# Attention probabilities laid out by key block, the sink as a column, reciprocals as a power on GpSimd: a Hymba-style streaming step in float32

## The chip, the core and the metric

One core of a Trainium2 chip runs one launch of the kernel. The metric is the device time of that launch in microseconds (us); lower is better. The engines are named as in the profile: PE is TensorE (PEld its weight loads), DVE is VectorE, ACT is ScalarE, POOL is GpSimd, SP is SyncE, which issues most DMAs. All data is float32, and 320 rows (256 of a prompt and 64 of a running stream) pass through one layer.

## The reference, cut to what matters

```python
z = rmsnorm(x, ln_g) @ w_in                      # 2048 -> 1024 q, 128 k, 128 v, 1024 u, 1024 v of the gating
# group A: 16 heads of 64, 2 key heads; a chunk of 64 queries sees its own 64 keys and the 128 before
s = einsum('...qhgd,...khd->...hgqk', q, k) * HEAD_DIM ** -0.5 + bias
sink = sinks[..., None]                          # one learned number per head
m = maximum(max(s, axis=-1), sink)
p = exp(s - m[..., None])
w = p / (sum(p, axis=-1, keepdims=True) + exp(sink - m)[..., None])
o = einsum('...hgqk,...khd->...qhgd', w, v)
# group B: spatial gating over chunks of 128 positions, 8 channel groups
u, v = gelu(zs)[..., :1024], rmsnorm(gelu(zs)[..., 1024:], g)
sp = einsum('gij,bnjgc->bnigc', masked w_s, v) + b_s
s_o = u * sp
# finish
x = x + concat(rmsnorm(o, g_a), rmsnorm(s_o, g_s)) @ w_out
y = x + square(relu(rmsnorm(x, ln_ffn) @ w_up)) @ w_down        # 2048 -> 8192 -> 2048
```

The outputs are `y` and the new rows of keys, values and of the normalised gating `v`.

## The kernel before

**Products.** Activations lie with channels on the 128 partitions and the 320 rows along the free dimension. Each product of a weight matrix is made by `products`: a step loads four 128 x 256 blocks of weights (`w_raw`), ACT copies them rounded to `w_hi` (line 115), DVE subtracts to get the rest, `w_lo` (line 116), and PE adds up three products for each block, high x high, high x low and low x high (line 141): 24 matmuls of 128x128 by 320 columns. `w_hi` and `w_lo` have three buffers each. The same split is made of the activations (`XH`, `XL` and so on). The stages follow each other: q and k, v of the attention (with the sums of squares `ssq` of the input, lines 285 to 292), the other q heads, the gating's `v` in four groups, its `u` in four groups, `w_out`, `w_up` and `w_down`.

**What stands between the steps.** `between_pieces` puts small work after a chosen step of a product. On PE it is pinned by `tc.issue_after`: the small matmuls stand behind the step's last matmul, and the next step stands behind them (`behind = narrow[-1]`). On the other engines a scheduler sets the order at build time; each engine then runs its list strictly in order.

**Attention.** A unit is one chunk of 64 queries for one key head, ten in all (5 chunks x 2 key heads; 64, 128 or 192 keys). `attend(i)` is called thirteen times (i = 0 to 12), every second step, and does one stage of three units at once:

- scores of unit i (`scores`, line 420): 8 products of 64x64 by 64 to 192 columns into two PSUM banks `s_ps`; then `softmax` on DVE, ACT and POOL;
- the transposes of the probabilities of unit i-2 (line 472) into two `misc` banks, from where DVE copies them to SBUF (`pts`, line 501);
- the values of unit i-3 (line 485): probabilities times values, 64x64 by 128 columns.

In `softmax` four DVE instructions scale and add the bias (line 434), DVE takes the maximum (438), joins the sink (440), negates (442) and forms sink minus maximum (444), ACT takes the exponent of that (445) and four exponents with row sums (449), DVE adds (451) and takes the reciprocal (452), and POOL multiplies the tile `s` in place (453). The tile `s` has two buffers. Probabilities are transposed in pieces of 128 rows x 128 columns that hold two key blocks; which value tiles they meet depends on the unit (`blocks`, with eight value tiles made by `values` from six transposes, line 349). A product of one key block and its partner in the same 128 rows lands in different places, so half of the results are added by DVE afterwards (line 497).

**Gating norm.** The channel factor `g_sv` of the gating's norm is multiplied on POOL into all 320 rows of `gv` (line 541), before the mixing matmuls (line 566); DVE then adds the bias `sgb` (line 571).

**Norm of q.** `norm_q` sums squares with four matmuls of 128x32 by 320 columns (line 323), sends the sums through DRAM to turn them, and raises to -0.5 on POOL (line 334).

Of the kernel before, what the change touches and what calls it, by code (L numbers as in the profile page):

```python
# [8 lines left out]
F32 = mybir.dt.float32  # L9
# [21 lines left out]
def hymba_step_kernel(ctx: ExitStack, tc: tile.TileContext, i, o):  # L31
# [53 lines left out]
    nc.gpsimd.dma_start(out=tab, in_=i["table"].rearrange("b h -> h b"))  # L85
    inv_1k = const.tile([P, 1], F32, name="inv_1k")
# [16 lines left out]
    loads, between, rests, steps, narrow, carry = [], [], [], [], [], []  # L103
# [18 lines left out]
    def products(w, k0, nk, c0, ps, rh, rl, deep=None, between_pieces={}, halves_behind={}):  # L122
# [6 lines left out]
        for a in range(0, nk, 4):  # L129
# [3 lines left out]
            with tc.issue_after(halves_behind[a // 4]()) if a // 4 in halves_behind else nullcontext():  # L133
                high, low = halves(raw, hi, lo)
# [166 lines left out]
    def evict_q(g, q_ps):  # L301
# [11 lines left out]
        nc.scalar.activation(out=sq, in_=qg, func=AF.Square)  # L313
        return sq

    q_dram = dram.tile([2, 2, 2, 2, T], F32, name="q_dram")
    r_at = lambda g, b, p: (g // 2) * 20 + p * 10 + (g % 2) * 5 + b

    def norm_q(h, sqs):

        st = misc()
        for c in range(4):
            mm = nc.tensor.matmul(out=st[c * 32:(c + 1) * 32, 0:T], lhsT=hone, rhs=sqs[c // 2][:, :, c % 2], start=True, stop=True)  # L323
# [14 lines left out]
    v0, v64, v128, vC, vD, w2, w3, w4 = (vz[:, x] for x in range(8))  # L338

# [4 lines left out]
    def values(*xs):  # L344
        for x, vps in zip(xs, [score_bank(1, "vps"), misc()] if len(xs) == 2 else banks(4)):
            t0 = (0, 64, 128, -64, 192, 256)[x]
            n = min(P, T - t0)
            with tc.issue_after(narrow[-1]):
                mm = nc.tensor.transpose(out=vps[0:n, 0:P], in_=kvx[:, 448 + t0:448 + t0 + n], identity=ident)
            narrow.append(mm.ins)  # L350
            for dst, r in (((v0, slice(0, P)), (w3, slice(HD, P))), ((v64, slice(0, P)),),
                           ((v128, slice(0, P)), (w2, slice(0, HD))), ((w2, slice(HD, P)),),
                           ((w3, slice(0, HD)), (vD, slice(HD, P))), ((w4, slice(0, HD)),))[x]:
                nc.vector.tensor_copy(out=dst[r], in_=vps[r, 0:P].rearrange("k (h d) -> k h d", h=2))


    q1_ps = product(w_in, 0, KT, 256, xh, xl, between_pieces={0: lambda: rstd(ssq, mean_dm, EPS, rx)},
                    halves_behind={2: lambda: rests[-1]})
# [5 lines left out]
    nc.scalar.activation(out=ksq, in_=zk, func=AF.Square)  # L364
    q0_sq = evict_q(0, q0_ps)
# [3 lines left out]
    def first_norms():  # L369
        rstd(ksq, mean_hd, EPS, rk)  # L370
        q1_sq.append(evict_q(1, q1_ps))

    def keys():
        for dst, c in ((kn[:, 0:256], slice(0, 256)), (kn[:, 384:448], slice(256, 320))):
            nc.vector.scalar_tensor_tensor(out=dst, in0=zk[:, c], scalar=g_k, in1=rk[:, c], op0=ALU.mult, op1=ALU.mult)
        for h in range(2):
# [8 lines left out]
        values(0, 1)  # L385

    q2_ps = product(w_in, 0, KT, 512, xh, xl,
                    between_pieces={0: first_norms, 1: lambda: norm_q(0, (q0_sq, q1_sq[0])), 2: keys, 3: lambda: values(2, 3, 4, 5)},
                    halves_behind={1: lambda: q0_out})
# [16 lines left out]
    room = blk("vnat", [P, 2432])  # L406
# [3 lines left out]
    pt1 = at.tile([P, 768], F32, name="pt1", bufs=1)  # L410
    pts = [(kzv[:, 1920:2304], room[:, 2048:2432]), (pt1[:, 0:384], pt1[:, 384:768])]
# [12 lines left out]
    def softmax(u, s_ps):  # L424
# [12 lines left out]
        m = at.tile([P, 2, 2], F32, name="m", tag="m")  # L437
        nc.vector.tensor_reduce(out=m, in_=sv, axis=AX.X, op=ALU.max)
        sk = sinks_pj[:, :, js]
# [310 lines left out]
```

## Time and profile before

| | |
|---|---|
| runs | 1239.65, 1239.93, 1240.73 us; median 1239.93 |
| profiled execution | 1239.04 us, of which 1237.3 are the span from first to last instruction |
| busy in the span | PE 1232.8 us, DVE 663.6, ACT 492.0, POOL 114.0 |
| granted TensorE clock | 1.0 throughout |
| DMA | 188.03 MB, mean 152 GB/s |

The span is cut into windows by the profile's time axis: the first product with q and k, v runs to about 34 us, the other q heads and the gating's `v` and `u` with the attention between them to about 212 us, and the rest is `w_out`, `w_up`, `w_down`. A row of the timeline has start and length in us, engine, line, operation, output<-input and shape; a bracket behind it is the time the engine sat idle before and what released it. In a group row (by line and shape) the numbers are busy us, mean ns of one, idle before. One matmul of float32 is listed as two records, a transpose and a matmul of the split operands as one.

### The profile page before, as it was taken

To read this page: it belongs to the slowest core of one execution; us is meant where nothing else is said; L and a number is where in the kernel's file an instruction comes from. 1 tells how busy PE (TensorE), PEld (TensorE's weight loads), DVE (VectorE), ACT (ScalarE), POOL (GpSimd) and SP (SyncE) were. 2 spreads that over 40 slices of the span, in tenths; PEclk is the share of its full clock that TensorE was granted. 3 is DMA by queue.
4 is the path that set the end of the run, shared out by engine and by line. 5 is a ranking of instruction groups with operands and counts; after the bars stand their busy time and mean duration, and the time that the engine had idled before them with its cause. 6 is when DMAs were issued, how large, how long until landed. Compare 5 with 4: busy or idle time off the path is not lost.

```text
span 1237.3 us, 20626 instructions
## 1 busy us (share of the span) xinstructions
PE 1232.8 (100%) x8666; PEld 1225.0 (99%) x8666; DVE 663.6 (54%) x796; ACT 492.0 (40%) x652; POOL 114.0 (9%) x139
## 2 busy tenths in 40 slices
PE   9999999999999999999999999999999999999998
PEld 9999999999999999999999999999999999999998
DVE  7877778877864444444444444444444434444343
ACT  7446566435534432333434332344432333433321
POOL 3127454102200000000000000000000000000000
PEclk9999999999999999999999999999999999999999
DMA  9753346444555444454444444455444454445540
GB/s 282 226 148 104 104 138 195 153 154 141 151 152 153 153 147 145 152 154 149 146 149 153 154 150 143 151 154 152 147 147 151 154 151 144 150 152 164 172 161 33
DMA packets 187934, 188.03 MB, mean 152 GB/s; under 512 B 7616, under 2 KB 187376, under 8 KB 187840
## 3 DMA queue, kind: packets, MB, share of 16 engines
q1 hardware_dynamic: 186544, 185.48, 48.7%
q0 software_dynamic: 864, 0.98, 0.4%
q8 instruction: 68, 1.11, 0.4%
q10 hardware_dynamic: 432, 0.24, 0.1%
q14 instruction: 26, 0.21, 0.1%
HBM read 183.10 MB, written 3.35 MB: 151 GB/s over the span
## 4 chain that ended last, share of the span: by engine, by line
PE 99%; DVE 0%; issue 0%; ACT 0%; DVEq 0%
PE acc L141 93%; PE q_ps L237 1%; PE misc L141 1%; PE acc L237 1%; PE s_ps L420 1%; PE misc L472 0%; PE misc L83 0%; PE misc L485 0%; PE s_ps L485 0%; PE g_ps L566 0%; PE misc L566 0%; PE misc L553 0%; PE misc L323 0%; ACT s L449 0%; ACT w_hi L115 0%
## 5 line engine op out<-in xcount | busy, mean ns | idle before, releaser
L116 DVE TENSOR_TENSOR w_lo<-w_raw,w_hi 128x1024 fp32r<-128x1024 f32 x332 | 416.0, 1253 | 422.7 <-ACT w_hi L115 414.1
L115 ACT ACTIVATE w_hi<-w_raw 128x1024 fp32r<-128x1024 f32 x332 | 351.8, 1060 | 670.9 <-PE acc L141 646.7
L141 PE MATMUL acc<-H2H,w_lo 128*128 128x320 f32 x1024 | 316.4, 309 | 0.0
L141 PE MATMUL acc<-H2H,w_hi 128*128 128x320 f32 x1024 | 316.4, 309 | 0.0
L141 PE MATMUL acc<-H2L,w_hi 128*128 128x320 f32 x1024 | 316.4, 309 | 0.0
L141 PE MATMUL acc<-FH,w_hi 128*128 128x320 f32 x992 | 306.5, 309 | 0.0
L141 PE MATMUL acc<-FL,w_hi 128*128 128x320 f32 x992 | 306.5, 309 | 0.0
L141 PE MATMUL acc<-FH,w_lo 128*128 128x320 f32 x992 | 306.5, 309 | 0.0
L141 PEld LDWEIGHTS acc<-H2H,w_hi 128*128 128x128 f32 x1024 | 192.2, 188 | 0.0
L141 PEld LDWEIGHTS acc<-H2L,w_hi 128*128 128x128 f32 x1024 | 192.2, 188 | 0.0
L141 PEld LDWEIGHTS acc<-H2H,w_lo 128*128 128x128 f32 x1024 | 192.2, 188 | 0.0
L141 PEld LDWEIGHTS acc<-FH,w_hi 128*128 128x128 f32 x992 | 186.2, 188 | 0.0
L141 PEld LDWEIGHTS acc<-FL,w_hi 128*128 128x128 f32 x992 | 186.2, 188 | 0.0
L141 PEld LDWEIGHTS acc<-FH,w_lo 128*128 128x128 f32 x992 | 186.2, 188 | 0.0
L141 PE MATMUL acc<-XH,w_hi 128*128 128x320 f32 x352 | 110.7, 314 | 0.0
L141 PE MATMUL acc<-XH,w_lo 128*128 128x320 f32 x352 | 108.8, 309 | 0.0
L141 PE MATMUL acc<-XL,w_hi 128*128 128x320 f32 x352 | 108.7, 309 | 0.0
L141 PEld LDWEIGHTS acc<-XH,w_hi 128*128 128x128 f32 x352 | 66.1, 188 | 3.1 <-issue 3.0
L141 PEld LDWEIGHTS acc<-XL,w_hi 128*128 128x128 f32 x352 | 66.1, 188 | 0.0
L141 PEld LDWEIGHTS acc<-XH,w_lo 128*128 128x128 f32 x352 | 66.1, 188 | 0.0
L658 DVE SCALAR_TENSOR_TENSOR tf<-acc,r 128x640 f32<-128x640 f32 x32 | 26.4, 824 | 41.8 <-PE acc L141 41.8
L673 DVE TENSOR_TENSOR xT<-xT,acc 128x640 f32<-128x640 f32 x31 | 25.5, 821 | 41.8 <-PE acc L141 41.8
(227 smaller groups left out, 1086.3 us busy)
## 6 DMA issues: line engine op xcount, KB each, us to landing
w_raw<-in_w_up SPq DMA_DIRECT2D x128, 512.0 KB
w_raw<-in_w_down SPq DMA_DIRECT2D x128, 512.0 KB
w_raw<-in_w_in SPq DMA_DIRECT2D x44, 512.0 KB
w_raw<-in_w_out SPq DMA_DIRECT2D x32, 512.0 KB
w_first<-in_w_in SPq DMA_DIRECT2D x14, 256.0 KB
out_yT<-xT SPq DMA_DIRECT2D x7, 320.0 KB
xT<-in_xT SPq DMA_DIRECT2D x8, 160.0 KB
xT<-in_xT SPq DMA_DIRECT2D x4, 320.0 KB
```

The source lines that it names most:

```text
L115: return (pin(nc.scalar.activation(out=hi, in_=raw, func=AF.Copy)).ins, pin(nc.vector.tensor_tensor(out=lo, in0=raw, in1=hi.bitcast(F32), ...
L116: pin(nc.vector.tensor_tensor(out=lo, in0=raw, in1=hi.bitcast(F32), op=ALU.subtract)).ins)
L141: mm = nc.tensor.matmul(out=out, lhsT=w_[:, k, g * P:(g + 1) * P], rhs=r_(kk), start=(kk == 0 and x == 0), stop=(kk == nk - 1 and x == 2))
L237: mm = nc.tensor.matmul(out=ps[:, 0:T], lhsT=w_[:, j, k, g * P:(g + 1) * P], rhs=r_(a + k), start=(a + k == 0 and x == 0), stop=(a + k == ...
L420: mm = nc.tensor.matmul(out=s_ps[p][x * HD:(x + 1) * HD, j * nk:(j + 1) * nk], lhsT=qT[hs, blk_, a + x], rhs=kz[hs, kv, k0:k0 + nk], start ...
L658: nc.vector.scalar_tensor_tensor(out=t, in0=ps[:, :, 0:T], scalar=0.0, in1=r2[:, None, :].to_broadcast([P, 2, T]), op0=ALU.max, op1=ALU.mult)
L673: nc.vector.tensor_tensor(out=xT[:, a, c], in0=xT[:, a, c], in1=p, op=ALU.add)
```

## The change

- **Probabilities by key block.** POOL writes the normalised probabilities to a new tile `pr`, laid out by key block (`p`, block `n`, head `j`, 64 keys), in two instructions for each unit. Each block is transposed by itself, separately for the two 64-query halves of the partitions: 64 rows x 128 columns in, 128 partitions x 64 columns out, the halves into two banks. The two value heads `j` then lie on the two halves of the partitions, so the values meet plain value tiles: 4 products for each key block, added up in one place for each `j`. The additions of line 497 go. The value tiles are seven, made from three transposes in one bank and four ACT copies (`values`, `values_out`) instead of six transposes and nine DVE copies; two DMAs instead of three bring the cached values.
- **The sink as a column.** `s` gets one more column that holds the sink; maximum (negated by the same instruction), exponent and row sum run over it. Lines 440, 442, 444, 445, 451 go; a DVE copy of 128x4 comes. `s` has one buffer instead of two.
- **Reciprocal.** A POOL power with exponent -1 (tile `minus`) replaces DVE's reciprocal.
- **Gating norm.** For the 256 prompt rows `g_sv` is no longer multiplied on POOL; DVE's addition of the bias becomes a multiply and add. For the 64 sample rows it stays on POOL.
- **Order.** Squares of the input start three steps earlier in the first product; the splits of the sums (`parts_x`, `parts_k`) are made ahead of the pieces that use them; `norm_q(1)` moves one step ahead, right behind `attend(2)`; the values of the first kind move to the piece of `norm_q(0)`.

```diff
-        with tc.issue_after(steps[min(8 + k // 2, 11)][0]):
+        with tc.issue_after(steps[min(5 + k // 2, 11)][0]):
...
-    def values(*xs):
-        for x, vps in zip(xs, [score_bank(1, "vps"), misc()] if len(xs) == 2 else banks(4)):
-            ...
-                mm = nc.tensor.transpose(out=vps[0:n, 0:P], in_=kvx[:, 448 + t0:448 + t0 + n], identity=ident)
-            ...
-                nc.vector.tensor_copy(out=dst[r], in_=vps[r, 0:P].rearrange("k (h d) -> k h d", h=2))
+    def values():
+        with tc.issue_after(narrow[-1]):
+            vps = score_bank(1, "vps").rearrange("k (x d) -> k x d", x=4)
+            for x, (t0, n) in enumerate(TT):
+                mm = nc.tensor.transpose(out=vps[0:n, x], in_=vT[:, t0:t0 + n], identity=ident)
+    def values_out():
+        for dst, to, of in ((low, 0, low), (high, 1, high), (high, 0, low), (low, 1, high)):
+            with tc.issue_after(turned[1]):
+                nc.scalar.activation(out=vz[dst, to:5:2].rearrange("k x h d -> k x (h d)"), in_=vps[of, 0:3 - to], func=AF.Copy)
...
-                    between_pieces={0: first_norms, 1: lambda: norm_q(0, (q0_sq, q1_sq[0])), 2: keys, 3: lambda: values(2, 3, 4, 5)},
+                    between_pieces={0: first_norms, 1: lambda: (values(), norm_q(0, (q0_sq, q1_sq[0])), values_out()), 2: keys},
...
-        s = at.tile([P, 2, 2, 192], F32, name="s", tag="s", bufs=2)
+        s = at.tile([P, 2, 2, 193], F32, name="s", tag="s", bufs=1)
+        sv, se = s[:, :, :, 0:nk], s[:, :, :, 0:nk + 1]
+        nc.vector.tensor_copy(out=s[:, :, :, nk], in_=sinks_pj[:, :, js])
         for p in range(2):
             for j in range(2):
                 nc.vector.scalar_tensor_tensor(out=sv[:, p, j], ...)
-        m = at.tile([P, 2, 2], F32, name="m", tag="m")
-        nc.vector.tensor_reduce(out=m, in_=sv, axis=AX.X, op=ALU.max)
-        nc.vector.tensor_tensor(out=m, in0=m, in1=sk, op=ALU.max)
-        nc.vector.tensor_scalar(out=nm, in0=m, scalar1=-1.0, scalar2=None, op0=ALU.mult)
-        nc.vector.tensor_tensor(out=es, in0=sk, in1=m, op=ALU.subtract)
-        nc.scalar.activation(out=es, in_=es, func=AF.Exp)
+        nc.vector.tensor_reduce(out=nm, in_=se, axis=AX.X, op=ALU.max, negate=True)
...
-                nc.scalar.activation(out=sv[:, p, j], in_=sv[:, p, j], func=AF.Exp, bias=nm[:, p, j:j + 1],
+                nc.scalar.activation(out=se[:, p, j], in_=se[:, p, j], func=AF.Exp, bias=nm[:, p, j:j + 1],
                                      accum_out=den[:, p, j:j + 1])
-        nc.vector.tensor_tensor(out=den, in0=den, in1=es, op=ALU.add)
-        nc.vector.reciprocal(out=den, in_=den)
-        ready[:] = [nc.gpsimd.tensor_tensor(out=sv, in0=sv, in1=den[:, :, :, None].to_broadcast([P, 2, 2, nk]),
-                                            op=ALU.mult).ins]
+        nc.gpsimd.tensor_tensor(out=den, in0=den, in1=minus, op=ALU.pow)
+        pr = at.tile([P, 2, 3, 2, HD], F32, name="pr", tag="pr", bufs=2)
+        for p in range(2):
+            ready[:] = [nc.gpsimd.tensor_tensor(out=pr[:, p, 0:ns].rearrange("x n j k -> x j n k"),
+                                                in0=sv[:, p].rearrange("x j (n k) -> x j n k", k=HD),
+                                                in1=den[:, p, :, None, None].to_broadcast([P, 2, ns, HD]), op=ALU.mult).ins]
...
+            def turn(p, n, x):
+                return nc.tensor.transpose(out=bank[x][:, (p * 3 + n) * HD:(p * 3 + n + 1) * HD],
+                                           in_=s[hs[x], p, n].rearrange("x j k -> x (j k)"), identity=ident[hs[x], hs[x]])
...
-                if va is not None:
-                    nc.vector.tensor_tensor(out=dst, in0=dst, in1=side[1 - j, j].rearrange("p (a q) -> p a q", a=2), op=ALU.add)
...
-            1: lambda: attend(2 * g + 2), 2: lambda: norm_q(1, (q2_sq, q3_sq)) if g == 0 else None,
-            3: lambda: attend(2 * g + 3)})
+            1: lambda: (attend(2 * g + 2), norm_q(1, (q2_sq, q3_sq)) if g == 0 else None), 3: lambda: attend(2 * g + 3)})
...
-            for dst, c in ((gv[:, a, 0:256], slice(0, 256)), (gvs[:, a], slice(256, T))):
-                with tc.issue_after(ready[0]) if g == 3 else nullcontext():
-                    nc.gpsimd.tensor_scalar(out=dst, in0=gv[:, a, c], scalar1=g_sv[:, a:a + 1], scalar2=None, op0=ALU.mult)
+            with tc.issue_after(ready[0]) if g == 3 else nullcontext():
+                nc.gpsimd.tensor_scalar(out=gvs[:, a], in0=gv[:, a, 256:T], scalar1=g_sv[:, a:a + 1], scalar2=None, op0=ALU.mult)
...
-            nc.vector.tensor_tensor(out=gv[:, g, 0:256].rearrange("p (b i) -> p b i", b=2),
-                                    in0=sp_ps[:, 0:256].rearrange("p (b i) -> p b i", b=2),
-                                    in1=sgb[:, g, None, :].to_broadcast([P, 2, P]), op=ALU.add)
+            nc.vector.scalar_tensor_tensor(out=gv[:, g, 0:256].rearrange("p (b i) -> p b i", b=2),
+                                           in0=sp_ps[:, 0:256].rearrange("p (b i) -> p b i", b=2), scalar=g_sv[:, g:g + 1],
+                                           in1=sgb[:, g, None, :].to_broadcast([P, 2, P]), op0=ALU.mult, op1=ALU.add)
```

On PE, `attend(10)` before: the last matmul of a step, six transposes of `s` in pieces of 128x128, the values (`pt` are transposed probabilities, `kzv` holds the value tiles) into four places, and the next step.

```order
L141 MATMUL acc<-XH,w_lo 128x320
L472 MATMUL misc<-ident,s 128x128 x6
L485 MATMUL misc<-pt_868,kzv 64x128 x2
L485 MATMUL s_ps_2096<-pt_868,kzv 64x128 x2
L485 MATMUL misc<-pt_868,kzv 64x128 x2
L485 MATMUL s_ps_2096<-pt_868,kzv 64x128 x2
L485 MATMUL s_ps_2095<-pt_868,kzv 64x128 x2
L485 MATMUL misc<-pt_868,kzv 64x128 x2
L141 MATMUL acc<-XH,w_hi 128x320
```

The same place now:

```order
L145 MATMUL acc<-XH,w_lo 128x320
L483 MATMUL misc<-ident,pr 128x64 x12
L493 MATMUL misc<-pt_856,kzv 64x128 x12
L145 MATMUL acc<-XH,w_hi 128x320
L145 MATMUL acc<-XL,w_hi 128x320
```

Twelve transposes with 64 columns out stand where six with 128 stood; the number of value products is the same, and they no longer touch the score banks. On DVE, around the softmax of unit 6 (128 keys; `z` and `gc` are the gelu's), before:

```order
L434 SCALAR_TENSOR_TENSOR s<-s_ps_1606,rq,bias 128x128 x2
L501 COPY kzv<-misc 128x384
L434 SCALAR_TENSOR_TENSOR s<-s_ps_1605,rq,bias 128x128 x2
L497 TENSOR_TENSOR ao<-ao,misc 128x2x64
L501 COPY vnat<-misc 128x384
L497 TENSOR_TENSOR ao<-ao,s_ps_1605 128x2x64
L438 TENSOR_REDUCE m<-s 128x4
L440 TENSOR_TENSOR m<-m,sinks 128x4
L442 TENSOR_SCALAR nm<-m 128x4
L444 TENSOR_TENSOR es<-sinks,m 128x4
L451 TENSOR_TENSOR den<-den,es 128x4
L452 RECIPROCAL den<-den 128x4
```

The same place now:

```order
L118 TENSOR_TENSOR w_lo<-w_raw,w_hi 128x1024
L444 COPY s<-sinks 128x4
L118 TENSOR_TENSOR w_lo<-w_raw,w_hi 128x1024
L447 SCALAR_TENSOR_TENSOR s<-s_ps_1582,rq,bias 128x128 x2
L447 SCALAR_TENSOR_TENSOR s<-s_ps_1583,rq,bias 128x128 x2
L451 TENSOR_REDUCE nm<-s 128x4
L506 COPY kzv<-misc 128x384 x2
L118 TENSOR_TENSOR w_lo<-w_raw,w_hi 128x1024
L444 COPY s<-sinks 128x4
```

The small instructions and the additions are gone; the copy of the sinks, which writes the only buffer of `s`, stands ahead of the next unit's four scalings, and both copies out of the transposes' banks stand behind those four. On POOL, units 3 and 4 (192 keys) before:

```order
L453 TENSOR_TENSOR s<-s,den 128x768
L334 TENSOR_TENSOR rq<-r_q,nhalf 128x20
L541 TENSOR_SCALAR gvs<-gv,cols 128x64 x2
L541 TENSOR_SCALAR gv<-gv,cols 128x256
L513 TENSOR_TENSOR acc_v<-acc_v,sq 128x320
L541 TENSOR_SCALAR gv<-gv,cols 128x256
L453 TENSOR_TENSOR s<-s,den 128x768
```

The same units now:

```order
L347 TENSOR_TENSOR rq<-r_q,nhalf 128x20
L545 TENSOR_SCALAR vnat<-gv,cols 128x64 x2
L457 TENSOR_TENSOR den<-den,minus 128x4
L519 TENSOR_TENSOR acc_v<-acc_v,sq 128x320
L461 TENSOR_TENSOR pr<-s,den 128x2x3x64 x2
L457 TENSOR_TENSOR den<-den,minus 128x4
L461 TENSOR_TENSOR pr<-s,den 128x2x3x64 x2
```

Each unit has a power and two multiplies in place of one multiply, and the power of unit 3 stands behind the `rq` power of `norm_q(1)`.

More of the change, by code (lines that the diff above doesn't have):

```diff
@@ L85, in hymba_step_kernel @@
     nc.gpsimd.dma_start(out=tab, in_=i["table"].rearrange("b h -> h b"))
+    minus = const.tile([P, 2, 2], F32, name="minus")
+    nc.vector.memset(minus, -1.0)
     inv_1k = const.tile([P, 1], F32, name="inv_1k")
@@ L100, in hymba_step_kernel @@
     nc.vector.memset(hone[HD:P, 1:2], 1.0)
-    loads, between, rests, steps, narrow, carry = [], [], [], [], [], []
+    firsts, loads, between, rests, steps, narrow, carry = [], [], [], [], [], [], []
     def load(out, in_):
@@ L405, in hymba_step_kernel @@
     probs, ready = {}, []
-    room = blk("vnat", [P, 2432])
+    room = blk("vnat", [P, 2560])
     vnat = room[:, 0:2048].rearrange("p (t c) -> p t c", t=2)
-    pt1 = at.tile([P, 768], F32, name="pt1", bufs=1)
-    pts = [(kzv[:, 1920:2304], room[:, 2048:2432]), (pt1[:, 0:384], pt1[:, 384:768])]
+    pts = [kzv[:, 1792:2560].rearrange("k (x p n q) -> k x p n q", x=2, p=2, n=3),
+           at.tile([P, 2, 2, 3, HD], F32, name="pt1", bufs=1)]
     def scores(u, s_ps):
@@ L460, in attend @@
         t, v = t if 0 <= t < 10 else None, v if 0 <= v < 10 else None
-        bank = [misc(), misc()] if t is not None else None
-        s_ps = [score_bank(p) for p in range(2)]
+        bank = [misc(), misc()] if t is not None else [score_bank(r) for r in range(2)]
+        s_ps = [score_bank(p) for p in range(2)] if i < 10 else None
+        hs = [slice(r * HD, (r + 1) * HD) for r in range(2)]
         def behind(mms):
@@ L468, in attend @@
         if t is not None:
-            s = probs.pop(t).rearrange("x p j k -> x p (j k)")
-            nk = blocks[units[t][0]][2]
-            cols = ((P, 2),) if nk == HD else ((0, 0), (192, 1)) if nk == P else ((0, 0), (256, 1), (P, 2))
-            behind([lambda p=p, x=x, c=c: nc.tensor.transpose(out=bank[p][:, x * P:(x + 1) * P], in_=s[:, p, c:c + P],
-                                                              identity=ident) for p in range(2) for c, x in cols])
+            s = probs.pop(t)
+            subs = range(len(blocks[units[t][0]][4]))
+            def turn(p, n, x):
+                return nc.tensor.transpose(out=bank[x][:, (p * 3 + n) * HD:(p * 3 + n + 1) * HD],
+                                           in_=s[hs[x], p, n].rearrange("x j k -> x (j k)"), identity=ident[hs[x], hs[x]])
+            behind([lambda p=p, n=n, x=x: turn(p, n, x) for p in range(2) for n in subs for x in range(2)])
         if i < 10:
@@ L477, in attend @@
             blk_, kv = units[v]
-            q0, va, vb = (blocks[blk_][x] for x in (0, 4, 5))
-            hs = [slice(r * HD, (r + 1) * HD) for r in range(2)]
-            side = {(r, j): bank[r][:, 384:512] if bank and j == 0 else s_ps[r][:, 384:512] if j else s_ps[r][:, 0:P]
-                    for r in range(2) for j in range(2)}
-            def part(r, j, p, span):
-                lhsT, c = (va[j][hs[r], kv], slice(j * P, (j + 1) * P)) if span < 2 else (vb[j][hs[j], kv], slice(256, 384))
-                return nc.tensor.matmul(out=side[r, j][hs[p]], lhsT=lhsT, rhs=pts[v % 2][p][hs[r], c],
-                                        start=span < 2 or va is None, stop=span == 2 or vb is None or r != j)
-            turns = [x for x in (0, 2, 1) if (va, va, vb)[x] is not None]
-            behind([lambda r=r, p=p, x=x: part(r, 1 - r if x == 1 else r, p, x) for x in turns for r in range(2) for p in range(2)])
+            q0, tiles = blocks[blk_][0], blocks[blk_][4]
+            side = [b[:, 384:512] for b in bank]
+            behind([lambda n=n, x=x, j=j, p=p: nc.tensor.matmul(out=side[j][hs[p]], lhsT=vz[hs[j], x, kv],
+                                                                rhs=pts[v % 2][hs[j], :, p, n], start=n == 0,
+                                                                stop=n == len(tiles) - 1)
+                    for n, x in enumerate(tiles) for j in range(2) for p in range(2)])
         if i < 10:
```

82 lines of the change are left out of this document (43 added, 39 removed).

## The prediction

> **What bounds the kernel now.** I read first the page's busy shares and its chain of work that ended last:
>
> ```profile
> PE 1232.8 (100%) x8666; PEld 1225.0 (99%) x8666; DVE 663.6 (54%) x796; ACT 492.0 (40%) x652; POOL 114.0 (9%) x139
> PE 99%; DVE 0%; issue 0%; ACT 0%; DVEq 0%
> ```
>
> TensorE sets the time. What DVE, ACT and POOL do counts only where PE has to wait for it. So two questions decide: does PE get less work of its own, and does a chain through the other engines become longer than the time between two pieces of PE work that it feeds? The windows by stage tell where there is room (start:end, span, then busy of PE, PEld, DVE, ACT, POOL, then clock):
>
> ```profile
> 5.00:34.00 29.00, 29.00 (x197) 29.00 (x197) 24.09 (x37) 22.87 (x37) 8.62 (x30) 1.00 0.99 298
> 34.00:64.00 30.00, 30.00 (x210) 29.28 (x209) 26.34 (x46) 12.64 (x16) 5.27 (x9) 1.00 0.73 211
> 64.00:168.00 104.00, 103.66 (x939) 98.43 (x941) 80.77 (x177) 57.46 (x154) 54.31 (x50) 1.00 0.44 121
> ```
>
> The attention lies in the third. PE is idle 0.34 us in 104 there, DVE is the fullest of the rest (78%). Then the chain again, in order of time (start, length, what):
>
> ```profile
> 78.42 0.60 PE s_ps L420 x16
> 86.47 0.81 PE s_ps L420 x16
> 90.99 0.68 PE misc L323 x8
> 104.08 0.66 PE misc L472 x6
> 113.22 0.66 PE misc L472 x6
> 161.62 0.97 ACT s L449 x5
> 162.59 0.96 ACT w_hi L115
> 164.33 1.59 issue
> ```
>
> One `attend` follows another after 113.22 - 104.08 = 9.14 us. Only the last one with transposes shows other engines in the chain: there PE waits for a copy that stands on DVE behind a weight split, behind ACT's exponents.
>
> **PE's own work.**
>
> ```profile
> L472 PE MATMUL misc<-ident,s 128*128 128x128 f32 x48 | 7.1, 273 | 0.3 <-DVE vnat L501 0.3
> L349 PE MATMUL misc<-ident,kvx 128*128 128x128 f32 x3 | 0.7, 272 | 0.0
> 103.91 0.82 PE L472 MATMUL misc<-ident,s 128*128 128x128 f32 x6
> 105.91 0.42 PE L141 MATMUL acc<-XH,w_hi 128*128 128x320 f32 x1
> 106.16 0.31 PE L141 MATMUL acc<-XL,w_hi 128*128 128x320 f32 x1
> 104.66 0.53 PEld L420 LDWEIGHTS s_ps<-kzv,qT 64*64 64x64 f32 x16 [0.17 <-issue]
> 105.91 0.19 PEld L141 LDWEIGHTS acc<-XH,w_hi 128*128 128x128 f32 x1 [0.17 <-issue]
> ```
>
> Matmuls overlap, so I take steps of the chain and not the mean of a record. Six transposes are 0.66 us, 0.11 each; 48 are 5.28 us. Now there are 96 with half the columns. From the chain, 64 more keys (0.60 to 0.81) cost 0.21 us for 16 records of which four run side by side, so 64 columns take 0.21 / 4 = 0.053 us, just half of 0.11. The two halves of the rows lie in separate tiles and into separate banks, as the score tiles do, so I let each pair run side by side at 0.055: 48 x 0.055 = 2.64, a saving of 2.6 us. Were they one after the other, 96 x 0.053 = 5.1, a saving of 0.2.
>
> Three transposes of values fewer: 3 x 0.11 = 0.33 us saved (the query lists three with this name, three others alike).
>
> Tile shapes: 128x128 to 64x64 stops the weight loads for 0.17 us, and so does the way back. `attend` now goes 128x128, 64x128, 64x64, 128x128, one change more. No row shows 64x128 to 64x64; by the two rows that there are I take 0.15 for each, ten times: 1.5 us lost. Ends: 0 and 1.7. The Trainium skill, "TensorEngine Tiling (Array Packing)", Key Properties, speaks against the change here: it says that changing the tiling mode, as opposed to the tile, drains TensorE. By that rule the loss is there, which agrees with the 0.17 us of the two shapes shown; without it PE's sum below would be -3.1 rather than -1.6.
>
> `norm_q(1)` has a piece of its own now (0.68 at 90.99, of 128x32 shape); right behind `attend(2)` it saves one return to 128x128: the first matmul after such a return takes 0.42 for 0.31, and its load stood still for 0.17, so some 0.2 us saved. Sum: -2.6 - 0.33 + 1.5 - 0.2 = **-1.6 us**, with -3.1 and +0.8 as ends.
>
> **The loop through the one buffer of s.** Before, DVE could fill the second `s` while POOL still multiplied the first. Now the copy of the sinks and the four scalings of the next unit wait until POOL's second multiply has read `s`. Behind them on DVE's list stand the copies out of the two transposes' banks, for which the next `attend`'s transposes on PE wait, and the weight splits `w_lo`. Rows of units 2 to 4:
>
> ```profile
> 98.02 1.39 DVE L434 SCALAR_TENSOR_TENSOR s<-s_ps,rq,bias 128x192 f32<-128x192 f32 x4
> 99.66 0.94 DVE L438 TENSOR_REDUCE m<-s 128x4 f32<-128x768 f32 x1
> 100.49 1.06 ACT L115 ACTIVATE w_hi<-w_raw 128x1024 fp32r<-128x1024 f32 x1 [0.71 <-PE acc L141]
> 101.46 0.44 ACT L449 ACTIVATE s<-s,nm 128x192 f32<-128x192 f32 x1
> 103.22 0.19 ACT L449 ACTIVATION_READ_ACCUMULATOR s<-s,nm 128x1 f32 x1
> 103.44 0.16 DVE L451 TENSOR_TENSOR den<-den,es 128x4 f32<-128x4 f32 x1 [0.63 <-ACT s L449]
> 109.26 0.54 DVE L501 COPY vnat<-misc 128x384 f32<-128x384 f32 x1
> 95.10 1.48 POOL L453 TENSOR_TENSOR s<-s,den 128x768 f32<-128x768 f32 x1
> 99.74 0.98 POOL L331 DMA_DIRECT2D r_q<-q_dram  x1
> 101.19 0.89 POOL L331 DMA_DIRECT2D r_q<-q_dram  x1 [0.47 <-DMA q_dram<-q_rows]
> 105.56 4.07 POOL L334 TENSOR_TENSOR rq<-r_q,nhalf 128x20 f32<-128x20 f32 x1
> ```
>
> ```profile
> L334 POOL TENSOR_TENSOR rq<-r_q,nhalf 128x20 f32<-128x20 f32 x2 | 7.6, 3820 | 2.0 <-DVE r_q L333 1.9
> L171 POOL TENSOR_TENSOR rs_rows<-r_rows,nhalf 128x3 f32<-128x3 f32 x1 | 1.8, 1792 | 0.5 <-DVE r_rows L169 0.5
> L453 POOL TENSOR_TENSOR s<-s,den 128x768 f32<-128x768 f32 x6 | 8.8, 1468 | 5.3 <-PE misc L485 3.3 <-DVE den L452 1.9
> 76.71 0.61 POOL L453 TENSOR_TENSOR s<-s,den 128x256 f32<-128x256 f32 x1 [4.87 <-DVE den L452]
> L513 POOL TENSOR_TENSOR acc_x<-acc_x,sq 128x320 f32<-128x320 f32 x15 | 16.7, 1112 | 88.5 <-ACT sq L512 87.9
> L541 POOL TENSOR_SCALAR gv<-gv,cols 128x256 f32<-128x256 f32 x8 | 8.8, 1112 | 0.0
> ```
>
> The power on four elements a partition: three take 1.79, twenty 3.82, so 0.12 an element and 1.9 us. Each of the two multiplies has 384: between 0.61 (256) and 1.47 (768), on the line 0.82. The ends are the same line and the `acc_x` row, 1.11 for only 320, as the new output goes by blocks of 64.
>
> One turn of the loop with 192 keys: copy of sinks 0.16 (as the row of 128x4), scalings 1.39, the two copies, which stand ahead of the maximum in units 3, 4, 8 and 9, 1.0, maximum 0.94, exponents 101.46 to 103.41 or 1.95, power 1.9, multiplies 1.64, and six hand-overs of about 0.1 (DVE 0.03 behind ACT, at 103.41 to 103.44, others longer): 9.6 us. On ACT a weight copy of 1.06 can stand ahead of the exponents, as at 100.49; half of it: 10.1. PE gives about 9.0 between two `attend`s after its saving. So each 192-key unit is late by some 1.1 us more, from 0 (no weight copy, shorter hand-overs) to 2.2.
>
> The start of it: unit 2's multiply began at 95.10; now the power (1.9) stands there and then the two issues of `r_q` (0.98 + 0.89), which `norm_q` one step ahead puts between power and multiplies on POOL's list. They end at 95.10 + 1.9 + 1.87 + 1.64 = 100.5, and unit 3's scalings begin at 100.7 instead of 98.02: 2.7 late. The power of 20 elements (4.07) then has until unit 3's exponents are done and costs nothing; otherwise up to 4 us once. The cover: the copy out of the banks ended at 109.80, PE needed the bank at 113.22, so 3.4 us. Lateness 2.7 at unit 3, 3.8 at unit 4, 4.9 at unit 5; above 3.4 PE waits: 1.5 us. Units 5 and 6 (64 and 128 keys) are shorter by an estimated 1.5 us for each 64 keys (two multiplies 0.42 less, the rest in proportion) and give back 1.9 + 0.4; lateness 1.1. Units 7 to 9 add 3.3, so 4.4, PE waits 1.0 at the last two `attend`s. Together **+2.5 us**, ends 0 and 9.
>
> **At nothing.** DVE's five small instructions and two additions per unit: off PE's path, and not in the turn above. Four ACT copies of values (each under the 1.06 of a weight copy) lie in the second window with ACT busy 12.64 of 30; without room, 4 us of late weights. Squares three steps earlier: the first window, PE 29.00 of 29.00, ACT 22.87; if they came ahead of a weight copy, a fraction of a microsecond once. The gating factor: POOL loses 8 x 1.11 = 8.9 us and gains 10 x 1.9 = 19 in a window where it is busy 54 of 104; DVE's instruction keeps its shape. One DMA fewer for cached values.
>
> **Sum.** 1239.04 - 1.6 + 2.5 = 1239.9 in a profiled execution. The median of the runs shown, 1239.93, is 0.9 above that execution; so **1240.8**. A change under 0.2%, 2.5 us, can't be told from none here (1237.45 to 1242.41).
>
> **Rivals.**
> - The loop fits: no weight copy ahead of the exponents, lateness stays below 3.4. For it: ACT is busy only 57.46 of 104. Then PE's sum decides: 1239.04 - 1.6 + 0.9 = 1238.3 (0.12, no change), or, if the extra tile shape is free as well, -3.1: 1236.8 (0.24, **faster**). That one decides when a turn stays within 9.2 us and a change costs under 0.07.
> - Multiplies slower, 1.1 each: 0.56 more per unit. Unit 3 is 3.3 late, unit 5 6.6, PE waits 3.2; later 3.8: 7.0 in all, 1239.04 - 1.6 + 7.0 + 0.9 = 1245.3 (0.18, **slower**). About 0.2 us more per unit is enough to pass 1242.4. For it the `acc_x` row, against it that 768 elements with the same broadcast took 1.47.
> - POOL's power holds up DVE's weight splits, as the multiplies do:
>
> ```profile
> 150.84 1.47 POOL L453 TENSOR_TENSOR s<-s,den 128x768 f32<-128x768 f32 x1 [3.30 <-PE misc L485]
> 151.24 2.15 DVE L116 TENSOR_TENSOR w_lo<-w_raw,w_hi 128x1024 fp32r<-128x1024 f32 x1 [0.57 <-ACT w_hi L115]
> 106.14 1.24 DVE L116 TENSOR_TENSOR w_lo<-w_raw,w_hi 128x1024 fp32r<-128x1024 f32 x1
> ```
>
>   Beside the multiply the split took 2.15 for 1.24. With 0.9 more per unit, PE would wait 9.7 by the same count: 1248.0. But beside the power at 105.56 it took 1.24, so 0.04. The Trainium skill, "SBUF — State Buffer", Who interferes with whom, says that a DVE instruction with two SBUF inputs contends with a GpSimd instruction that reads SBUF, the loser blocked for the whole of it; the 2.15 agrees, the 1.24 beside 4.07 us of power does not.
> - Transposes not side by side: 2.4 more on PE, but the loop gets 0.25 more per `attend`, so about 1.1 net: 1241.9, at the bound (0.09, half of it slower).
>
> That nothing happens because DVE's removed work was hidden anyway is part of the first.
>
> **Chances.** The forecast, loop slightly too long and PE saving most of it back, 0.33, with a range of its own from 1238.5 to 1242.4. Faster 0.24; same 0.33 + 0.12 + 0.05 = 0.50; slower 0.18 + 0.04 + 0.04 = 0.26. The range runs from the free tile shape to the slower multiplies, 1236.5 to 1245.3.
>
> **What would show it.** In the chain, the transposes of a 192-key unit at 0.33 for 0.66. A gap in the weight loads between transposes and what follows them. POOL's power at 1.9, multiplies at 0.8. DVE's scalings released by POOL's multiply from unit 3 on, and PE idle 1.5 us at the `attend`s around unit 5 and 1.0 at the last, released by DVE's copies. I am wrong if the last `attend`s show no such idle time, or if several us are lost at each.

## The result and the profile after

The changed kernel takes 1241.32 us, median of 22 runs (1240.62 to 1242.03); the kernel before, run beside it, 1239.66 (22 runs). The ratio is 1.0013, 95% interval 1.0007 to 1.0019: 1.7 us slower, inside what was called no change, and 0.5 us from the forecast of 1240.8. Taken as a change the forecast was +0.9 (1240.8 against 1239.93), so about half of what came. The profiled execution spans 1239.1 us (before 1237.3).

Busy shares, the chain by engine, and the window of the attention, each now:

```profile
PE 1232.5 (99%) x8711; PEld 1223.4 (99%) x8711; DVE 649.9 (52%) x732; ACT 490.9 (40%) x646; POOL 128.7 (10%) x151
PE 94%; POOL 3%; issue 2%; DVE 1%; DMA 0%; ACT 0%; SPq 0%; POOLq 0%; DVEq 0%
64.00:168.00 104.00, 101.64 (x960) 95.52 (x959) 66.27 (x115) 53.76 (x142) 64.46 (x57) 1.00 0.42 116
```

DVE lost 14.5 us in that window, POOL gained 10, and PE is idle 2.36 us where it was idle 0.34. POOL is in the chain for the first time. What PE waited for:

```profile
PE misc L483 <- DVE pt L506: 1.7, 2, 1.1
PE misc L483 <- DVE kzv L506: 0.2, 1, 0.2
```

These are the transposes, which wait for DVE's copies out of their banks, as forecast. (The list holds only the time in which PE itself stood idle ahead of a group. Its weight loads wait too, at attend 6 another 0.27 us for the copy out of the second bank, so less is listed than is lost.) The chain up to attend 6, in order of time, walks along the turn of the loop from POOL to DVE to PE; its first row, an "issue" on POOL, stands in place of unit 4's scalings, maximum and exponents:

```profile
110.33 5.31 issue
115.68 1.02 POOL den L457
116.77 3.60 POOL pr L461 x2
120.37 0.02 issue
120.39 0.17 DVE s L444
120.56 0.76 DVE s L447 x4
121.32 0.40 DVE gc L527
121.72 0.94 DVE pt L506 x2
122.66 0.04 issue
122.71 0.59 PE misc L483 x9
```

and DVE's scalings of units 4 and 5 stand one turn apart, each right behind the release by POOL:

```profile
110.36 0.17 DVE L444 COPY s<-sinks 128x4 f32<-128x4 f32 x1 [1.50 <-POOL pr L461]
110.44 1.39 DVE L447 SCALAR_TENSOR_TENSOR s<-s_ps,rq,bias 128x192 f32<-128x192 f32 x4
120.39 0.17 DVE L444 COPY s<-sinks 128x4 f32<-128x4 f32 x1 [0.72 <-POOL pr L461]
120.47 0.85 DVE L447 SCALAR_TENSOR_TENSOR s<-s_ps,rq,bias 128x64 f32<-128x64 f32 x4
```

120.47 - 110.44 = 10.03 us; the forecast turn was 10.1. Its parts are other ones:

```profile
L461 POOL TENSOR_TENSOR pr<-s,den 128x384 f32<-128x384 f32 x12 | 17.7, 1495 | 0.3
L457 POOL TENSOR_TENSOR den<-den,minus 128x4 f32<-128x4 f32 x10 | 10.2, 1019 | 27.3 <-ACT s L455 26.0 <-PE misc L493 1.3
```

The power takes 1.02 us, not 1.9; a pair of multiplies of 192 keys 2.5 to 3.6, not 1.64.

### The profile page after: what moved, and what is told of

Same layout as the page of the kernel before. It is cut to its first block, busy times and chain, and to the rows that moved or that the text cites. A ratio compares the mean times of both kernels' runs of the same rounds, so it can differ in the third digit from the quotient of the medians.

```text
span 1239.1 us, 20639 instructions
## 1 busy us (share of the span) xinstructions
PE 1232.5 (99%) x8711; PEld 1223.4 (99%) x8711; DVE 649.9 (52%) x732; ACT 490.9 (40%) x646; POOL 128.7 (10%) x151
## 4 chain that ended last, share of the span: by engine, by line
PE 94%; POOL 3%; issue 2%; DVE 1%; DMA 0%; ACT 0%; SPq 0%; POOLq 0%; DVEq 0%
PE acc L145 89%; POOL pr L461 1%; PE q_ps L245 1%; PE misc L145 1%; PE acc L245 1%; POOL den L457 0%; POOL vnat L545 0%; POOL acc_v L519 0%; DVE s L447 0%; POOL gc L528 0%; DMA w_first<-in_w_in 0%; PE s_ps L434 0%; DVE w_lo L118 0%; PE misc L493 0%; POOL q_dram L341 0%
```

## The experiments

Theory L: the turn through the one buffer `s`, together with its late start at unit 3, makes DVE's copies late, and PE waits. Rival P: POOL itself, with power and multiplies, makes the probabilities late. Each was timed beside the kernel before on the same chip, and that took 1239.53 to 1239.92 us; so a few tenths between the times of two of these kernels show nothing. 1241.32 is the changed kernel, at 1.0007 to 1.0019 of the time before.

**Two buffers of s, one of pr.**

```diff
-        s = at.tile([P, 2, 2, 193], F32, name="s", tag="s", bufs=1)
+        s = at.tile([P, 2, 2, 193], F32, name="s", tag="s", bufs=2)
-        pr = at.tile([P, 2, 3, 2, HD], F32, name="pr", tag="pr", bufs=2)
+        pr = at.tile([P, 2, 3, 2, HD], F32, name="pr", tag="pr", bufs=1)
```

> The changed kernel with two buffers of s and one of pr (the same room). Theory L (the turn through the one s makes the copies out of the banks late): DVE's scalings no longer wait for POOL's second multiply, PE's waits at the transposes (0.6, 1.1, 0.4 and 1.5 us at attend 5, 6, 9 and 10) go to under 0.3 in all, and the time falls by 3.0 to 3.5 us below the changed kernel, to about 1238.0. Rival P (POOL's longer chain of power and multiplies itself makes the probabilities late for PE): the waits stay, under 1 us gained, 1240.5 or more.

1241.94 us (ratio 1.0021, 1.0013 to 1.0030): nothing gained, as rival P said. But the run doesn't decide, since `pr` has one buffer less and the order on POOL moved too. Unit 5's multiplies now began 5.2 us after the end of their power, with other work between:

```profile
122.24 1.01 POOL L457 TENSOR_TENSOR den<-den,minus 128x4 f32<-128x4 f32 x1 [0.83 <-ACT s L455]
123.74 1.91 POOL L545 TENSOR_SCALAR vnat<-gv,cols 128x64 f32<-128x64 f32 x2 [0.50 <-DVE gv L530]
125.61 2.87 POOL L519 TENSOR_TENSOR acc_v<-acc_v,sq 128x320 f32<-128x320 f32 x2
128.44 0.75 POOL L461 TENSOR_TENSOR pr<-s,den 128x128 f32<-128x128 f32 x2
```

and PE waited 1.1 us for `pr` and 1.9 for DVE's copies. It was repeated in a form that keeps POOL's order (below).

**DVE's reciprocal instead of the power.**

```diff
-        nc.gpsimd.tensor_tensor(out=den, in0=den, in1=minus, op=ALU.pow)
+        nc.vector.reciprocal(out=den, in_=den)
```

> The changed kernel with DVE's reciprocal in place of POOL's power. Theory L: the turn of a 192-key unit is shorter by 1.02 (power) less 0.18 (reciprocal), so about 9.2 us instead of 10.05, near the time between two attends; the waits shrink to 0 to 1 us, time 1238.3 to 1239.3. Rival: DVE now stands waiting for ACT's exponents with the weight splits behind it, and loses as much: 1241 or more.

1238.19 us (0.9990, 0.9981 to 0.9999): 3.1 less than the changed kernel. The time was as L said, the turn was not: units 4 and 5 begin at 109.31 and 119.39, still 10.1 apart. POOL is done with `s` earlier, but DVE has a weight split ahead of the scalings:

```profile
114.82 2.59 POOL L461 TENSOR_TENSOR pr<-s,den 128x384 f32<-128x384 f32 x2 [5.45 <-DVE den L457]
118.26 1.22 DVE L118 TENSOR_TENSOR w_lo<-w_raw,w_hi 128x1024 fp32r<-128x1024 f32 x1
119.39 0.85 DVE L447 SCALAR_TENSOR_TENSOR s<-s_ps,rq,bias 128x64 f32<-128x64 f32 x4
```

What changed is the start, see the table behind the runs. Not all of that is the reciprocal's own: POOL's list moved as well, one of the two issues of `r_q` (0.94 us) now standing behind unit 2's multiplies.

**One multiply in the old order of elements** (the values then meet probabilities of other keys; all sizes stay).

```diff
-        for p in range(2):
-            ready[:] = [nc.gpsimd.tensor_tensor(out=pr[:, p, 0:ns].rearrange("x n j k -> x j n k"),
...
+        ready[:] = [nc.gpsimd.tensor_tensor(out=pr.rearrange("x p n j k -> x p (n j k)")[:, :, 0:2 * nk].rearrange(
+                                                "x p (j k) -> x p j k", j=2),
+                                            in0=sv, in1=den[:, :, :, None].to_broadcast([P, 2, 2, nk]), op=ALU.mult).ins]
```

> The changed kernel with one multiply for each unit that writes the probabilities in the old order of elements, without the reordering by key block (so the values meet probabilities of other keys; all else has its size and place). If the reordered output or the halving makes the multiplies slow (2.5 to 3.6 us a pair), one instruction takes 1.5 and the turn is 1.1 to 2 us shorter, under 9 us: the waits go, time about 1238. If they are slow only because of DVE beside them, the instruction takes 2 us or more, the turn shortens by half a us, and the time falls by 1 to 2 us.

1240.53 us (1.0009, 1.0000 to 1.0018), 0.8 less, near the second case, though the intervals overlap. What decides is the trace. Where the one multiply took 1.5 us, DVE's weight split waited in its place (the two begin too close together for the records to say which came first); where the split had begun 0.26 us before it, the multiply took 2.45:

```profile
96.27 1.48 POOL L460 TENSOR_TENSOR pr<-s,den 128x768 f32<-128x768 f32 x1
96.15 2.69 DVE L118 TENSOR_TENSOR w_lo<-w_raw,w_hi 128x1024 fp32r<-128x1024 f32 x1
107.98 2.45 POOL L460 TENSOR_TENSOR pr<-s,den 128x768 f32<-128x768 f32 x1
107.72 1.38 DVE L118 TENSOR_TENSOR w_lo<-w_raw,w_hi 128x1024 fp32r<-128x1024 f32 x1 [0.44 <-ACT w_hi L117]
```

So neither the new order of elements nor the halving is the main cost, but DVE's weight split beside it. The pair shows the same in steps of about 1 us; first in the run with the reciprocal (no split beside it, then one), then in the changed kernel (two splits):

```profile
95.22 1.61 POOL L461 TENSOR_TENSOR pr<-s,den 128x384 f32<-128x384 f32 x2
150.62 2.59 POOL L461 TENSOR_TENSOR pr<-s,den 128x384 f32<-128x384 f32 x2 [3.04 <-PE misc L493]
151.25 1.27 DVE L118 TENSOR_TENSOR w_lo<-w_raw,w_hi 128x1024 fp32r<-128x1024 f32 x1 [0.77 <-ACT w_hi L117]
```

```profile
116.77 3.59 POOL L461 TENSOR_TENSOR pr<-s,den 128x384 f32<-128x384 f32 x2
116.58 1.23 DVE L118 TENSOR_TENSOR w_lo<-w_raw,w_hi 128x1024 fp32r<-128x1024 f32 x1 [2.96 <-ACT w_hi L117]
118.46 1.22 DVE L118 TENSOR_TENSOR w_lo<-w_raw,w_hi 128x1024 fp32r<-128x1024 f32 x1
```

The page "SBUF — State Buffer" of the Trainium skill, Who interferes with whom, says that of a DVE instruction with two SBUF inputs and a GpSimd one that reads SBUF, whichever begins first keeps the other out to its end. The multiplies and the splits agree where the records show which came first (2.45 and 3.59 us).

**Full transposes**, with the changed kernel and then with the reciprocal.

```diff
-                return nc.tensor.transpose(out=bank[x][:, (p * 3 + n) * HD:(p * 3 + n + 1) * HD],
-                                           in_=s[hs[x], p, n].rearrange("x j k -> x (j k)"), identity=ident[hs[x], hs[x]])
+                return nc.tensor.transpose(out=bank[p][:, n * P:(n + 1) * P],
+                                           in_=s[:, p, n].rearrange("x j k -> x (j k)"), identity=ident)
...
-                                      in_=bank[x][:, 0:384].rearrange("k (p n q) -> k p n q", p=2, n=3)[:, :, ns])
+                                      in_=bank[p][:, 0:384].rearrange("k (n x q) -> k x n q", x=2, n=3)[:, :, ns])
```

> The changed kernel with each key block transposed in one pass of 128 rows x 128 columns in place of two tiles of 64 x 128 (six passes for a 192-key unit, no change of tile shape between step and transposes). By the prediction's terms PE pays 2.6 us more for the passes and 1.5 less for the shape: +1.1 in all where PE doesn't wait. By the measured pieces (attend 4: 2.106 us before, 1.963 now) it is +0.14 for each of six units and nothing for the others: +0.8. As PE waits in four of the attends anyway, the time rises by 0 to 0.8, to 1241.3 to 1242.1. Rival (the two halves don't run side by side and the new form costs as much): no change or a fall.

> Full 128x128 transposes as in the fourth run, now with DVE's reciprocal, where PE waits for nothing: the worth of the 64x128 transposes alone, against the run with the reciprocal (1238.19). By the prediction's terms +1.1 (2.6 less 1.5): 1239.3. By the measured pieces (+0.14 in each of six units, +0.05 in two of four passes, less in the shortest): +0.8, 1239.0. If nothing but the waits told them apart in the fourth run: 1238.2.

1242.56 us (1.0024, 1.0015 to 1.0034) with the power, 1238.58 (0.9991, 0.9982 to 0.9999) with the reciprocal, that is 1.2 and 0.4 us more than without. In both cases the intervals overlap, so the times don't show it. The 1.2 is beyond the 0 to 0.8 expected, and it isn't the transposes alone: in its trace another instruction (`acc_v`) stands between power and multiplies of unit 5, and attend 7 takes 1.3 us longer than with the reciprocal. The chains with the reciprocal, at attends where PE waits for nothing, do show what the transposes cost. Tiles of 64x128 (12, 8 and 4 passes), then full ones (6, 4 and 2):

```profile
104.02 0.52 PE misc L483 x12
95.36 0.40 PE misc L483 x8
86.38 0.27 PE misc L483 x4
```

```profile
113.20 0.66 PE misc L483 x6
95.36 0.44 PE misc L483 x4
86.42 0.22 PE misc L483 x2
```

From 4 to 12 passes it is 0.25 us, 0.031 a pass, with 0.145 us fixed: so the halves do run side by side, a pair costs 0.063 where one full pass costs 0.11, and the extra tile shape costs 0.145, read as the part that doesn't grow with the passes. With two key blocks or more the new form wins (0.14 us for three), with one it loses 0.05. Over the ten units that is 0.85; only 0.4 came because the run with 64x128 tiles still loses some 0.55 at two attends (table below) and the one with full tiles loses nothing there. Attend 4 of the changed kernel shows where the weight loads stop: 0.19 us ahead of the transposes, and hardly (103.64 to 103.71) between them and the scores:

```profile
103.19 0.45 PEld L483 LDWEIGHTS misc<-ident,pr 64*128 64x128 f32 x12 [0.19 <-issue]
103.71 0.53 PEld L434 LDWEIGHTS s_ps<-kzv,qT 64*64 64x64 f32 x16
```

**Two s, POOL's order kept.** The second `s` lies in unused columns behind `kvx`; the sinks' copy is pinned behind the unit's own scalings.

```diff
-    kvx = blk("kvx", [P, 768])
+    kvx = blk("kvx", [P, 1540])
...
+        if u % 2:
+            s = kvx[:, 768:1540].rearrange("x (p j k) -> x p j k", p=2, j=2)
+        else:
+            s = at.tile([P, 2, 2, 193], F32, name="s", tag="s", bufs=1)
-        nc.vector.tensor_copy(out=s[:, :, :, nk], in_=sinks_pj[:, :, js])
...
+        with tc.issue_after(last.ins):
+            nc.vector.tensor_copy(out=s[:, :, :, nk], in_=sinks_pj[:, :, js])
```

> The changed kernel with a second s (in the unused columns behind kvx), two pr as in the changed kernel, the copy of the sinks pinned behind the unit's own scalings; GpSimd's list stays in the changed kernel's order, which the first run with two s did not leave. Theory L (the turn through the one s): the scalings and the copies out of the banks come some 3 us earlier from unit 4 on, PE's waits of 3.5 us in all go to under 0.5, time 1238.0 to 1238.8. Rival P (POOL's power and multiplies are the late ones in any case): PE then waits for pr itself, little gained, 1240.5 or more.

1238.18 us (0.9988, 0.9979 to 0.9997): 3.1 less than the changed kernel, as L said. (The two edits, the second `s` and the later copy of the sinks, weren't told apart; one wait stayed, 0.7 us at attend 10, where under 0.5 in all was expected.) Power and multiplies are as slow as before, unit 4's pair again 3.59:

```profile
112.97 3.59 POOL L465 TENSOR_TENSOR pr<-s,den 128x384 f32<-128x384 f32 x2
115.78 0.85 DVE L449 SCALAR_TENSOR_TENSOR kvx<-s_ps,rq,bias 128x64 f32<-128x64 f32 x4
```

but unit 5's scalings begin at 115.78, before that pair ends at 116.56. Rival P falls.

**norm_q(1) in a piece of its own again.**

```diff
-            1: lambda: (attend(2 * g + 2), norm_q(1, (q2_sq, q3_sq)) if g == 0 else None), 3: lambda: attend(2 * g + 3)})
+            1: lambda: attend(2 * g + 2), 2: lambda: norm_q(1, (q2_sq, q3_sq)) if g == 0 else None,
+            3: lambda: attend(2 * g + 3)})
```

> The changed kernel with norm_q(1) again in a piece of its own, one step later. PE pays the return to 128x128 that the change saves: +0.2. On GpSimd the two issues of r_q (1.87 us) no longer stand between power and multiplies of unit 2, so unit 3's scalings start 1.5 to 2 us earlier; but the power of 20 elements (4 us) now comes after unit 3's multiplies or delays unit 4's. If the late start counts: PE's waits at attend 5 and 6 (1.6 us) go, time 1240.0 to 1240.5. If the turn makes up for any start: only the +0.2, 1241.5.

1240.05 us (1.0005, 0.9997 to 1.0014), 1.3 less than the changed kernel, but the intervals overlap. The traces show that the late start counts, in part: unit 3 begins 2 us earlier, and the losses at attend 5 (0.6) and 9 (0.4) go; the one at attend 6, which was to go as well, stays at 1.4. Moving `norm_q` ahead, which saves PE 0.2 us, cost some 1.1 elsewhere by these losses.

**Channel factor on GpSimd for all rows again**, with one `s` and with two.

```diff
-                nc.gpsimd.tensor_scalar(out=gvs[:, a], in0=gv[:, a, 256:T], scalar1=g_sv[:, a:a + 1], scalar2=None, op0=ALU.mult)
+            for dst, c in ((gv[:, a, 0:256], slice(0, 256)), (gvs[:, a], slice(256, T))):
...
+                    nc.gpsimd.tensor_scalar(out=dst, in0=gv[:, a, c], scalar1=g_sv[:, a:a + 1], scalar2=None, op0=ALU.mult)
```

> The changed kernel with the gating norm's channel factor on GpSimd for all rows again (8 instructions of 1.11 us more there, DVE's bias addition as before). The prediction counted this part at nothing: 1241.0 to 1241.6. If GpSimd's list is what makes the turn long, the instructions that stand ahead of a power or a multiply make the waits longer by 1 us or more: 1242.3 or more.

> The fifth run's kernel (two s, sinks' copy behind the scalings) with the channel factor on GpSimd for all rows again. If the 5.1 us that this part cost with one s came through the turn (instructions of 0.9 to 3.9 us between power and multiplies make s free late), most of it is absorbed by the second s: 1238.2 plus the 1.2 us for which PE waited at the transposes of gv, 1238.5 to 1240.5. If GpSimd's list is the limit by itself, the 5 us stay: 1243.

With one `s` 1246.44 us (1.0061, 1.0048 to 1.0075): 5.1 more than the changed kernel. With two 1239.79 (0.9999, 0.9990 to 1.0008): only 1.6 more than without. In the first, the scalings of `gv` stand on POOL between a unit's power and its multiplies, where `s` is still held. They do so for unit 3 (two of 0.92 us) and, at the highest price, for unit 5, behind which attend 7 loses 2.8 us where the changed kernel loses 0.1:

```profile
126.19 1.04 POOL L457 TENSOR_TENSOR den<-den,minus 128x4 f32<-128x4 f32 x1
127.20 0.88 POOL L519 TENSOR_TENSOR acc_v<-acc_v,sq 128x320 f32<-128x320 f32 x1
128.06 3.85 POOL L546 TENSOR_SCALAR gv<-gv,cols 128x256 f32<-128x256 f32 x2
131.89 0.75 POOL L461 TENSOR_TENSOR pr<-s,den 128x128 f32<-128x128 f32 x2
```

What is left with two `s` is mostly one wait of PE at the transposes of `gv`, which the first has as well (1.2):

```profile
PE misc L562 <- ACT vnat L564: 1.3, 1, 1.3
```

**Two s and the reciprocal** (both edits above).

> Two s and DVE's reciprocal together. Each alone takes 3.1 us off the changed kernel. If both remove the same thing (PE's waits for the turn), the two together give nothing more: 1237.8 to 1238.2, PE's own work. If they were separate costs: about 1235.1.

1238.27 us (0.9987, 0.9978 to 0.9996), the same as each alone. Both take away the same thing, and what is left is PE's own work, but for some 0.5 us still lost at attend 10.

**The power with another exponent** (the probabilities are then divided by the root of their sum).

```diff
-    nc.vector.memset(minus, -1.0)
+    nc.vector.memset(minus, -0.5)
```

> The changed kernel with the exponent -0.5 in place of -1 (the probabilities are divided by the root of their sum; all else is the same). The prediction took the power on 4 elements as 1.9 us, on a line through 1.79 (3 elements) and 3.82 (20), both with exponent -0.5; it took 1.02. If the exponent tells them apart, the power takes 1.8 to 2 us here, and the time rises by some 3 to 6 us. If not, it stays at 1.02 us and 1241.

One run of each: 1241.25 us, before 1239.80. The power stays as it was, so the exponent isn't what set my estimate wrong. What did is shown in the next section. By group, in this run:

```profile
L457 POOL TENSOR_TENSOR den<-den,minus 128x4 f32<-128x4 f32 x10 | 10.2, 1021 | 27.3 <-ACT s L455 26.0 <-PE misc L493 1.3
```

**The runs together.** The table joins them. It gives how late a unit's scalings begin, counted from the first matmul of the step behind its `attend` (from the timelines of DVE and PE, us), and what PE loses at the next `attend`: the length of its small work there beyond the shortest seen in these runs.

| kernel | unit 3 | 4 | 5 | 7 | 8 | 9 | lost after 4, 5, 8, 9 |
|---|---|---|---|---|---|---|---|
| before | 1.2 | 1.4 | 2.1 | 3.5 | 3.7 | 4.8 | 0, 0, 0, 0 |
| changed | 4.5 | 5.5 | 6.1 | 4.3 | 5.5 | 6.4 | 0.6, 1.1, 0.4, 1.5 |
| reciprocal | 1.8 | 3.6 | 4.9 | 3.0 | 4.1 | 5.2 | 0, 0.2, 0, 0.35 |
| two s, order kept | 2.3 | 1.4 | 1.9 | 1.7 | 4.4 | 5.6 | 0, 0, 0, 0.7 |
| norm_q apart | 2.5 | 4.7 | 6.0 | 3.6 | 5.0 | 6.3 | 0, 1.4, 0, 1.4 |

Up to about 5 us lateness costs nothing; beyond that PE loses roughly the excess. (Before, 0.5 us was lost at attend 11, which is gone now.)

## Why the prediction came out right

**PE's own work, -1.6:** -1.4 by the chains. Transposes 96 x 0.031 + 10 x 0.145 = 4.4 us against 5.3, so -0.85 where -1.1 was counted: the pair costs 0.063, not 0.055; the extra shape 0.145, counted as 0.15. A unit's transposes came to 0.52 us, where 0.33 was named as the sign. The value transposes take 0.33 us in the chain now and 0.66 before (0.22 at 59.58, 0.44 at 63.31). From attend 2 to attend 3 with `norm_q(1)` it is 8.94 us in the run with the reciprocal and full transposes and 9.13 before, so its 0.2 is there as well. Tile changes do cost, so the rival in which the shape is free is out, and the halves are side by side.

**The loop, +2.5:** the place was right (DVE held by POOL's multiply, PE waiting for the copies around units 5 and 9), the size too low. Lost after units 4 and 5: 0.6 + 1.1 = 1.7 us, forecast 1.5; after 8 and 9: 0.4 + 1.5 = 1.9, forecast 1.0. The old loss of 0.5 was left standing in the forecast and went. Net of it, with 0.3 at attend 7 and 8: 3.9 - 0.5 = 3.4 for 2.5. With PE's -1.4 that is +2.0, against +1.7 of the medians.

The first half of this sum fits the mechanism: unit 5 began 4.0 us later than before with 0.6 lost already, 4.6 for the forecast 4.9. The second half came out for another reason. The forecast had unit 9 late by 4.4 with 3.4 us of cover. By the table unit 9 began 1.6 later than before, 2.0 with the loss ahead of it, but there the kernel before already stood at 4.8 of the 5 us that cost nothing: cover 0.2, not 3.4.

Two prices in the turn were wrong and cancelled, which was luck. The power: 1.02 us, not the 1.9 drawn through a row of 3 and one of 20 elements; 20 elements alone, at 0.2 each, would have given 0.8. The false point was the row of 3, which holds a weight split too. In the kernel before, the split had begun 0.16 us ahead of that power and ended at 179.52; the power ended 0.74 later, 0.25 an element, as 1.02 is for four:

```profile
178.47 1.79 POOL L171 TENSOR_TENSOR rs_rows<-r_rows,nhalf 128x3 f32<-128x3 f32 x1 [0.50 <-DVE r_rows L169]
178.31 1.21 DVE L116 TENSOR_TENSOR w_lo<-w_raw,w_hi 128x1024 fp32r<-128x1024 f32 x1
```

The changed kernel has the same pair (180.67 and 180.51); no run took the split away. The pair of multiplies: its own time is the 1.61 forecast, but one or two weight splits get in ahead of it, 1 us each. Smaller parts were off as well: unit 4's turn has no weight copy ahead of its exponents, where half of one, 0.53, was counted. The third rival spoke of this contention, but had it with the power, and with the power as the one that blocks: beside a power already running the split kept its 1.24 us (106.14, in the prediction's rows). The second rival's price, 1.1 a multiply or 2.2 a pair, came nearer to what the pair took, for another reason. By the count of the rivals, where 0.56 us more per unit made 4.5 us, either alone would have moved the forecast out of its own range.

**The late start, 2.7 at unit 3:** it was 3.2 (in the table unit 3 goes from 1.24 to 4.45 before rounding; the 100.41 of the trace stands near the forecast 100.7 only because this execution runs 0.8 us ahead of the other at that step). Counted from that step, the power began 1.2 us sooner than the multiply did before, and it took 1.03 us instead of 1.9; the `r_q` issues came between, with 1.87, as said. Against that stand a pair of 2.8, not 1.64, and a copy of the sinks that took 1.53 us beside POOL's multiply of `gc` and not 0.16:

```profile
94.12 1.87 POOL L344 DMA_DIRECT2D r_q<-q_dram  x2
96.00 2.81 POOL L461 TENSOR_TENSOR pr<-s,den 128x384 f32<-128x384 f32 x2
98.78 1.57 POOL L528 TENSOR_TENSOR gc<-gc,z 128x640 f32<-128x640 f32 x1
98.85 1.53 DVE L444 COPY s<-sinks 128x4 f32<-128x4 f32 x1 [0.71 <-POOL pr L461]
```

**At nothing, the gating factor:** right for the change as a whole, wrong as a reason. It was weighed by POOL's busy share, 54 of 104 us; but it kept instructions out of the gap between power and multiplies, and without it the same change costs 5.1 us more, of which some 1.5 are at the transposes of `gv` and the rest in the turn. The other items at nothing (values copied by ACT, earlier squares, small DVE instructions) were not tried.

**The better kernel:** with two `s` in POOL's order, or with the reciprocal left on DVE, the change gains: 0.9988 (0.9979 to 0.9997) and 0.9990 (0.9981 to 0.9999) of the time before.

## What to carry to other kernels

When a double buffer is given up, write out the turn of the loop that now closes, from one engine's release to the next, and compare it and its start with the time between two uses: a lateness below the cover is free, above it nearly every microsecond counts. Weigh work on an off-path engine by where it stands in its list, not by its busy share; here one buffer alone, or the slower reciprocal alone, cost nothing that the times show, and both together 3.1 us. Before a price is drawn through two rows, look at what the other engines did beside them. An experiment on buffers has to show that the order of the other engines stayed.

## What was unexpected on the hardware

- A power on 128x4 elements on POOL took 1.02 us, the same with exponents -1 and -0.5. On 128x20, in the changed kernel, it took 3.56 us at 100.58, with no weight split running when it began, and 4.48 at 68.46, where a split had begun at 68.28; the 1.79 of 128x3 holds such a split too. So a split holds back a power that comes after it, while a power already running leaves the split its 1.24 us.
- Splitting one POOL multiply into two let DVE's weight splits in, ahead of either half: 1.61 us for the pair alone, 2.59 with one, 3.59 with two.
- A DVE copy of 128x4 took 1.53 us beside POOL's multiply where alone it takes 0.17, and ended when that multiply did (98.78 + 1.57 = 100.35, 98.85 + 1.53 = 100.38).
